# Two-layer transformer backbone: the first two token pairs of the second layer are normalised and transposed during the first layer's attention and parked in DRAM

## The chip, the cores and the metric

The kernel runs on one core of a Trainium2 chip. The metric is the device time of one execution in microseconds (us); of several executions the median is taken.

## The reference

The reference is a backbone of two layers over 256 context tokens and 1024 latent tokens, each 1024 wide. Layer 0 is a windowed attention, layer 1 a latent attention. Cut to what matters here, with layer 1's input normalisation in the first line of the loop:

```python
for i in range(DEPTH):                       # DEPTH = 2
    hx = rms_norm(x, norm_g[i]) * (1.0 + scale_x) + shift_x
    hc = rms_norm(ctx, norm_g[i]) * (1.0 + scale_c) + shift_c
    yx, yc = window_gqa(hx, hc, ...) if i == 0 else latent_attention(hx, hc, ...)
    x = x + gate_x * yx
    if i < DEPTH - 1:
        ctx = ctx + gate_c * yc
return rms_norm(x, final_g)
# latent_attention begins with
cq, ckv, kr, g = split(h @ w_in)             # for the latent and the context tokens
```

All arithmetic is in float32. Products on TensorE (PE) are made from operands split into a high and a low part: the helper mm3 (L124 to L128) issues three matmuls for one product, and the helper split (L119 to L122) makes the parts, a cast on ScalarE (ACT, L121) and a subtraction (L122) on VectorE (DVE) or GpSimd (POOL).

## The kernel before

The 1280 tokens are ten tiles of 128, called t0 to t9 here; t0 and t1 are the context, and two neighbouring tiles are a pair (p0 is t0 and t1, p4 is t8 and t9). Most of SBUF is two arenas, arena_f (plain numbers) and arena_r (split operands), in which every stage has fixed places, given in KB per partition. A ring is a list of such places that are taken in turn; whoever takes a place waits until its last user is done.

**Layer 0's attention** runs in 40 units, one for each tile and each of 4 head groups, in the tile order 2, 0, 3, 1, 4, 5, 6, 7, 8, 9. A unit's work is written out by hand: scores (PE, L586), masked and reduced on DVE (L597), exponentials on ACT (L600), transposes of the probabilities through the two PSUM banks 6 and 7 (PE, L617), a split of what was transposed (L121, L122), the product with V (PE, L627), and a normalisation of the unit's output (L637 to L654, fin and fin2, whose transposes are L646). Behind four units stands the output product of their tile, outproj: mm3 calls that are handed out piece by piece inside the next tile's units, then L674 and L675, and the finished tile goes to DRAM in x1_d (L676). The last tile's outproj has no unit left to hide in and runs after the last unit.

**Layer 1's beginning** (from the line fetch1(0, nc.vector) on) makes its inputs from x1_d. For a tile, norm_x loads it (L212), squares and sums it on ACT (L214), makes the reciprocal root in three small steps (L215 DVE, L216 POOL), and scales it (L217 DVE); turn_x transposes it in eight 128x128 blocks on PE (L224), four to a PSUM bank, and copies the two banks out on ACT (L225). For a pair, build_h applies the layer's scale and shift (L238 DVE, eight a pair), and splits it (L241 ACT, L243 DVE) into hT1, the operand of the products. Then kv_tile computes each tile's key/value latents, 24 matmuls over 288 columns, with a squared sum on ACT (L958), small steps (L959 DVE, L960 POOL), a scaling on DVE (L997), and, two tiles later, a transpose and a split of the result (L1010, L121, L122), and g_tile(6, p) a part of the gates, 48 matmuls over 256 columns.

The weights come through a staging ring of three places, stg: fetch1 loads a piece (L264), splits it (L121, L122), and only then may the place be loaded again. Block 0 (the kv weights, eight pieces of 144 KB) is split by ACT and DVE, blocks 6 and 1 (four pieces of 256 KB each, here W6 and W1) by ACT and POOL. All loads named here are issued by the SP queue, in its order: an issue that must wait for a place holds up those behind it.

The program text gives the order of effects; a scheduler puts the instructions of the five engines into queues of its own choosing, up to the second layer's attention, whose PE, ACT and DVE order is written by hand. In such a queue nothing overtakes.

Of the kernel before, what the change touches and what calls it, by code (L numbers as in the profile page):

```python
# [18 lines left out]
D = 1024  # L19
# [41 lines left out]
def kernel(ctx: ExitStack, tc: tile.TileContext, t, out, dbg=None):  # L61
# [14 lines left out]
    x1_d = dpool.tile([TOK, D], F32, name="x1_d")  # L76
    qn_d = dpool.tile([8, 128, 2, SEQ], F32, name="qn_d")
# [132 lines left out]
    def norm_x(src, xr, junk):  # L210
        x = xr.next()
        load(out=x, in_=src)  # L212
        st = sm_ring()
# [4 lines left out]
        return x  # L218

    def turn_x(x, xt, j):  # L220
        for q in range(2):
            ps = shp(pst(), 4, 128)
            for c in range(4):
                nc.tensor.transpose(ps[:, c, :], x[:, (4 * q + c) * 128 : (4 * q + c + 1) * 128], ident)  # L224
            nc.scalar.copy(xt[:, 4 * q : 4 * q + 4, j * 128 : j * 128 + 128], ps)  # L225

    def build_x(p, src, xr, xtr, junk):

        xt = shp(xtr.next(), 8, 256)
        for j in range(2):  # L230
            turn_x(norm_x(src(2 * p + j), xr, junk), xt, j)
        return xt

    def build_h(p, xt, hT, A, B, fast=False, ks=range(8)):

        w = 1 if p == 0 else 0
        for k in ks:
            nc.vector.tensor_scalar(xt[:, k, :], xt[:, k, :], A[:, k, w : w + 1], B[:, k, w : w + 1], ALU.mult, ALU.add)  # L238
            if k % 2:
                hi = hT[:, 0, k - 1 : k + 1, :]  # L240
                nc.scalar.copy(hi, xt[:, k - 1 : k + 1, :])  # L241
                eng = nc.vector if fast or k % 4 == 1 else nc.gpsimd
                eng.tensor_sub(hT[:, 1, k - 1 : k + 1, :], xt[:, k - 1 : k + 1, :], hi.bitcast(F32))  # L243
# [434 lines left out]
    units = [UnitA(ti, g) for ti in ORDER for g in range(4)]  # L678

# [193 lines left out]
    for ui, u in enumerate(units):  # L873
# [11 lines left out]
        for ci in range(u.m):  # L885
# [215 lines left out]
    for ti in range(NT):  # L1101
        n = ti + 3
        if 4 <= n < NT:
            if n % 2 == 0:
                xt = shp(xtr.next(), 8, 256)
# [16 lines left out]
    qst = Ring(F, [16, 20, 24, 37, 41, 45], 1024)  # L1122
# [553 lines left out]
```

## Time and profile before

| what | us |
|---|---|
| median of 3 executions (1597.37 to 1597.9) | 1597.49 |
| profiled execution, its own time | 1596.15 |
| its span, first to last instruction | 1594.4 |
| around the span | 1.75 |

PE is busy for 1555.2 us of the span (98%), DVE for 905.9, ACT for 777.0 and POOL for 742.1. The mean granted PE clock is 0.997 of full speed. Layer 0's attention lies at about 360 to 716 us, layer 1's beginning after it. In the rows of the timeline the first number is the start in us from the span's start, the second the time in us of the instructions that the row merges, and a bracket gives the idle time before it and what ended that. Matmuls overlap, so that the distance from row to row, not the time in a row, is what a matmul takes.

### The profile page before, as it was taken

To read this page: it belongs to the slowest core of one execution; us is meant where nothing else is said; L and a number is where in the kernel's file an instruction comes from. 1 tells how busy PE (TensorE), PEld (TensorE's weight loads), DVE (VectorE), ACT (ScalarE), POOL (GpSimd) and SP (SyncE) were. 2 spreads that over 40 slices of the span, in tenths; PEclk is the share of its full clock that TensorE was granted. 3 is DMA by queue.
4 is the path that set the end of the run, shared out by engine and by line. 5 is a ranking of instruction groups with operands and counts; after the bars stand their busy time and mean duration, and the time that the engine had idled before them with its cause. 6 is when DMAs were issued, how large, how long until landed. Compare 5 with 4: busy or idle time off the path is not lost.

```text
span 1594.4 us, 26916 instructions
## 1 busy us (share of the span) xinstructions
PE 1555.2 (98%) x9938; PEld 1222.6 (77%) x9938; DVE 905.9 (57%) x1629; ACT 777.0 (49%) x1478; POOL 742.1 (47%) x805
## 2 busy tenths in 40 slices
PE   7899999999999999998999999999999999999998
PEld 4787777887878888887998899766766766766687
DVE  3515551618777777768525302667677677667454
ACT  3522232348777777767523332455545555555322
POOL 1231112115664444454113350388688688689510
PEclk9999999999999999999999999999999999999999
DMA  7446776354333333327113753313232233244251
GB/s 253 166 138 196 233 210 190 97 153 120 109 110 94 97 93 94 93 79 244 35 34 106 262 184 94 103 30 101 69 96 80 76 88 96 67 130 118 67 167 66
DMA packets 147203, 192.82 MB, mean 121 GB/s; under 512 B 13936, under 2 KB 84080, under 8 KB 147072
## 3 DMA queue, kind: packets, MB, share of 16 engines
q1 hardware_dynamic: 145456, 188.94, 39.5%
q10 hardware_dynamic: 1616, 2.17, 0.5%
q8 instruction: 78, 1.28, 0.4%
q14 instruction: 53, 0.43, 0.1%
HBM read 144.90 MB, written 46.15 MB: 120 GB/s over the span
## 4 chain that ended last, share of the span: by engine, by line
PE 86%; issue 2%; DVE 2%; POOL 2%; ACT 2%; DMA 1%; SPq 0%; POOLq 0%; DVEq 0%; ACTq 0%
PE PB L126 15%; PE PB L127 14%; PE PB L128 14%; PE PB L1303 11%; PE PB L1325 8%; PE PB L586 5%; PE PB L627 4%; PE PB L1266 4%; PE PB L617 4%; PE PB L183 1%; PE PB L1274 1%; PE PB L1354 1%; PE PB L646 1%; ACT arena_r L121 1%; DVE arena_r L122 1%
## 5 line engine op out<-in xcount | busy, mean ns | idle before, releaser
L126 PE MATMUL PB<-arena_r 128*128 128x512 f32 (+3 forms) x1496 | 509.9, 342 | 4.9 <-POOL arena_r L653 2.0
L127 PE MATMUL PB<-arena_r 128*128 128x512 f32 (+3 forms) x1496 | 502.4, 336 | 4.2 <-DVE arena_r L390 2.1
L128 PE MATMUL PB<-arena_r 128*128 128x512 f32 (+3 forms) x1496 | 500.3, 335 | 0.3 <-DVE arena_r L122 0.3
L1317 POOL TENSOR_TENSOR arena_f<-arena_f 128x512 f32<-128x512 f32 x252 | 328.3, 1303 | 82.1 <-ACT arena_f L1309 65.3
L126 PEld LDWEIGHTS PB<-arena_r 128*128 128x128 f32 x1496 | 283.7, 190 | 52.7 <-issue 12.5
L127 PEld LDWEIGHTS PB<-arena_r 128*128 128x128 f32 x1496 | 284.5, 190 | 32.0 <-DVE arena_r L390 3.5
L128 PEld LDWEIGHTS PB<-arena_r 128*128 128x128 f32 x1496 | 284.5, 190 | 28.3 <-DVE arena_r L122 0.5
L122 POOL TENSOR_TENSOR arena_r<-arena_f,arena_r 128x512 fp32r<-128x512 f32 x88 | 115.2, 1325 | 299.7 <-ACT arena_r L121 255.5
L1309 ACT ACTIVATE arena_f<-PB 128x1024 f32<-128x1024 f32 x160 | 164.1, 1027 | 108.9 <-PE PB L1303 65.9
L1268 DVE TENSOR_REDUCE arena_f<-PB 128x1 f32<-128x1024 f32 x128 | 156.1, 1219 | 86.7 <-PE PB L1266 86.6
L1303 PE MATMUL PB<-arena_r 64*128 64x512 f32 (+1 forms) x1600 | 202.3, 392 | 0.3 <-ACT arena_f L1309 0.3
L1303 PEld LDWEIGHTS PB<-arena_r 64*128 64x128 f32 (+1 forms) x1600 | 146.1, 185 | 31.5 <-ACT arena_f L1309 1.8
L122 DVE TENSOR_TENSOR arena_r<-PB,arena_r 128x512 fp32r<-128x512 f32 (+1 forms) x186 | 124.2, 674 | 61.9 <-ACT arena_r L121 61.0
L1325 PE MATMUL PB<-arena_f 128*64 128x512 f32 x640 | 144.4, 597 | 0.0
L600 ACT ACTIVATE arena_f<-arena_f,small 128x640 f32<-128x640 f32 (+2 forms) x160 | 119.5, 747 | 35.4 <-DVE small L597 32.7
L597 DVE CUSTOM_DVE_ANT_0 arena_f<-PB,arena_f,small 128x640 f32<-128x640 f32 (+2 forms) x176 | 125.2, 722 | 20.1 <-PE PB L586 12.6
L121 ACT CAST arena_r<-PB 128x512 fp32r<-128x512 f32 (+1 forms) x186 | 105.3, 573 | 47.4 <-PE PB L617 45.2
L121 ACT CAST arena_r<-arena_f 128x512 fp32r<-128x512 f32 (+3 forms) x141 | 83.8, 603 | 86.7 <-PE PB L128 12.5
L627 PE MATMUL PB<-arena_r 128*128 128x512 f32 x336 | 115.8, 429 | 0.5 <-DVE arena_f L639 0.5
L586 PE MATMUL PB<-arena_r 128*128 128x256 f32 (+1 forms) x576 | 111.0, 308 | 1.6 <-DVE small L597 1.3
L1325 PEld LDWEIGHTS PB<-arena_f 128*64 128x64 f32 x640 | 43.1, 136 | 83.2 <-issue 79.9
L617 PE MATMUL PB<-ident,arena_f 128*128 128x128 f32 x672 | 104.2, 274 | 1.3 <-DVE arena_r L122 0.8
(177 smaller groups left out, 1842.9 us busy)
## 6 DMA issues: line engine op xcount, KB each, us to landing
arena_f<-ada_w SPq DMA_DIRECT2D x47, 512.0 KB, 5.4
arena_r<-q_d SPq DMA_DIRECT2D x80, 256.0 KB, 3.9
arena_r<-qn_d SPq DMA_DIRECT2D x64, 256.0 KB, 3.9
arena_r<-qr_d SPq DMA_DIRECT2D x192, 64.0 KB, 3.3
arena_f<-a_w_in SPq DMA_DIRECT2D x40, 256.0 KB, 3.6
arena_f<-x SPq DMA_DIRECT2D x16, 512.0 KB, 6.6
g_d<-arena_f SPq DMA_DIRECT2D x32, 256.0 KB, 2.1
q_d<-arena_f SPq DMA_DIRECT2D x64, 128.0 KB, 2.4
```

What stands on the lines that cost most here:

```text
L121: nc.scalar.copy(hi, src)
L122: (lo_eng or nc.vector).tensor_sub(lo, src, hi.bitcast(F32))
L126: nc.tensor.matmul(o, ah, bh, start=first, stop=False)
L127: nc.tensor.matmul(o, al, bh, start=False, stop=False)
L128: nc.tensor.matmul(o, ah, bl, start=False, stop=last)
L586: nc.tensor.matmul(S[:, at : at + n], qT[:, s, hq, :], kT[:, g, k : k + n], start=s == 0, stop=s == 1)
L617: nc.tensor.transpose(pt[:, h, :], self.Ps[h][:, ci * 128 : ci * 128 + 128], ident)
L627: nc.tensor.matmul(self.pv, V[:, self.chunks[ci], self.g, :], PT[:, s], start=ci == 0 and s == 0, stop=ci == self.m - 1 and s == 1,)
L1303: nc.tensor.matmul(S[:, t], k[r, c : c + 128], q[r], start=j == 0, stop=j == 4)
L1309: nc.scalar.activation(E, self.S, AF.Exp)
L1317: eng.tensor_add(self.acc, self.acc, E[:, t])
L1325: nc.tensor.matmul(self.pv[p : p + 64], Vq[:, cs[t], self.h % 4, :], E[:, t], start=i == 0, stop=i == 4)
```

## The change

The first two pairs (t0 to t3) no longer go through norm_x and turn_x in layer 1. A generator, pre_turns, does the same work during layer 0's attention, tile by tile, four steps a tile and one step after each of the units 20 to 35 (tiles t5 to t8 of the attention); the results go to DRAM (xT_d), and load_xt brings them back, pair 0 during unit 38, pair 1 at the beginning of layer 1. In between, several rings are moved: layer 0's gr, or1 and rtr, layer 1's stg (its third place from 49.5 to 34 KB), xr, junk and the ring xtr, which becomes two fixed pairs of places, xt_at. The same instructions as before stay for pairs 2, 3 and 4.

```diff
+    xT_d = dpool.tile([2, 128, 8, 256], F32, name="xT_d")
...
-    or1, rtr = (Ring(F, [o, o - 5], 256) for o in (43, 45))
+    or1, rtr = Ring(F, [43, 44], 256), Ring(F, [45, 41], 256)
-    gr = Ring(F, [2.5, 34, 46], 256)
+    gr = Ring(F, [34, 35, 46], 256)
...
+    xpre, tpre = f_at(48, 1024), [f_at(o, 4, 128) for o in (36, 38)]
+    def pre_turn(ti):
+        load(out=xpre, in_=x1_d[ti * 128 : ti * 128 + 128, :])
+        yield
+        st = sm(4)
+        nc.scalar.activation(f_at(36, 512).bitcast(BF16), xpre, AF.Square, accum_out=st[:, 0:1])
+        nc.gpsimd.tensor_scalar(st[:, 1:2], st[:, 0:1], 1.0 / D, EPS, ALU.mult, ALU.add)
+        nc.gpsimd.tensor_tensor(st[:, 2:3], st[:, 1:2], mhalf, ALU.pow)
+        yield
+        nc.vector.tensor_scalar_mul(xpre, xpre, st[:, 2:3])
+        yield
+        for q in range(2):
+            ps = shp(pst3(), 4, 128)
+            for c in range(4):
+                k = 4 * q + c
+                nc.tensor.transpose(ps[:, c, :], xpre[:, k * 128 : k * 128 + 128], ident)
+            nc.scalar.copy(tpre[q], ps)
+            ts = slice(ti % 2 * 128, ti % 2 * 128 + 128)
+            load(out=xT_d[ti // 2, :, 4 * q : 4 * q + 4, ts], in_=tpre[q])
+        yield
+    xt_at = [[f_at(o, 4, 256) for o in os] for os in ((48, 36), (14, 18))]
+    def load_xt(p):
+        for q in range(2):
+            load(out=xt_at[p][q], in_=xT_d[p, :, 4 * q : 4 * q + 4, :])
...
+        if 20 <= ui < 36:
+            next(pre)
+        if ui == 38:
+            load_xt(0)
...
-    junk = f_at(34.5, 512).bitcast(BF16)
-    stg = Ring(F, [30, 32.25, 49.5], 576)
-    xr = Ring(F, [22, 26, 45], 1024)
-    xtr = Ring(F, [14, 37], 2048)
+    junk = f_at(40, 512).bitcast(BF16)
+    stg = Ring(F, [30, 32, 34], 512)
+    xr = Ring(F, [22, 26, 42], 1024)
...
     fetch1(0, nc.vector)
-    xts = {0: build_x(0, src1, xr, xtr, junk)}
-    build_h(0, xts.pop(0), hT1[0], ada1.A, ada1.B, fast=True)
-    xts[1] = build_x(1, src1, xr, xtr, junk)
-    build_h(1, xts.pop(1), hT1[1], ada1.A, ada1.B, fast=True)
+    load_xt(1)
+    build_h(0, xt_at[0], hT1[0], ada1.A, ada1.B, fast=True)
+    build_h(1, xt_at[1], hT1[1], ada1.A, ada1.B, fast=True)
```

The scheduler lays the queues anew. In the changed kernel the helpers' lines are one further on (the cast of split is L122, its subtraction L123) and norm_x and turn_x stand at L213, L219 to L222 and L228, L229. Three places matter for what follows.

On ACT, behind the last unit, before the change: the casts of the kv weights (L121, 128x288) alternate with the squares (L214) and the copies of the transposed tiles (L225) of t0 to t3; the squares are those of t0, t1 and t2.

```order
L121 CAST arena_r<-arena_f 128x288 x3
L214 ACTIVATE arena_f<-arena_f 128x1024 x2
L121 CAST arena_r<-arena_f 128x288 x2
L225 COPY arena_f<-PB 128x4x128
L121 CAST arena_r<-arena_f 128x288
L225 COPY arena_f<-PB 128x4x128 x2
L214 ACTIVATE arena_f<-arena_f 128x1024
```

On ACT at the same place with the change: the first square (L219) is t4's, the second t5's, and between them stand the last kv weights, the copies of t4, the first two casts of W6 (L122, 128x512) and the squared sum of kv tile 0 (L993).

```order
L122 CAST arena_r<-arena_f 128x288 x2
L219 ACTIVATE arena_f,small<-arena_f 128x1024
L122 CAST arena_r<-arena_f 128x288 x5
L1006 DMA arena_f<-b_q_norm 128x512
L122 CAST arena_r<-arena_f 128x288
L229 COPY arena_f<-PB 128x4x128 x2
L1008 DMA arena_f<-b_kv_norm 128x256
L122 CAST arena_r<-arena_f 128x512 x2
L993 ACTIVATE arena_f,small<-PB 128x256
L219 ACTIVATE arena_f,small<-arena_f 128x1024
L122 CAST arena_r<-arena_f 128x512
```

So t0 to t3 are gone from ACT's queue there, t4 has moved to the front, and t5 stands behind two weight casts that wait for transfers.

On SP with the change, from the end of unit 38 on: the loads of the turned pair 1 (L708), then the tiles t4, t5 and t6 (L213) between the pieces of the kv weights (L263, 128x288), the store of t8 of layer 0 (L675), the reload of t9 for the last output product (L657) and the first two pieces of W6 (L263, 128x2x256).

```order
L708 DMA arena_f<-xT_d 128x1024 x2
L213 DMA arena_f<-x_d 128x1024
L263 DMA arena_f<-b_w_in 128x288 x2
L213 DMA arena_f<-x_d 128x1024
L675 DMA x_d<-arena_f 128x1024
L263 DMA arena_f<-b_w_in 128x288 x3
L657 DMA arena_f<-x 128x1024
L213 DMA arena_f<-x_d 128x1024
L263 DMA arena_f<-b_w_in 128x288 x3
L263 DMA arena_f<-b_w_in 128x2x256 x2
```

Before the change the tiles loaded in this stretch were t0 to t4, and one piece of the kv weights stood much farther ahead, in front of the store of an earlier tile; now all eight stand here.

On ACT in the attention, at unit 23 and alike at units 27, 31 and 35, the copies of a turned tile (L695) stand right behind the unit's own output copies (L636) and ahead of its exponentials (L599), of the next output copy (L647) and of the next cast of transposed probabilities (L122).

```order
L636 COPY arena_f<-PB 64x256 x2
L695 COPY arena_f<-PB 128x512 x2
L599 ACTIVATE arena_f,small<-arena_f,small 128x640
L647 COPY arena_f<-PB 128x256
L122 CAST arena_r<-PB 128x512
```

Before, the cast of transposed probabilities that now follows later stood in the place of L695.

More of the change, by code (lines that the diff above doesn't have):

```diff
@@ L224, in turn_x @@
                 nc.tensor.transpose(ps[:, c, :], x[:, (4 * q + c) * 128 : (4 * q + c + 1) * 128], ident)
[L225 to L232, printed above, removed]
+            nc.scalar.copy(xt[q][:, :, j * 128 : j * 128 + 128], ps)
     def build_h(p, xt, hT, A, B, fast=False, ks=range(8)):
@@ L1103 @@
         if 4 <= n < NT:
-            if n % 2 == 0:
-                xt = shp(xtr.next(), 8, 256)
+            xt = xt_at[n // 2 % 2]
             turn_x(nx, xt, n % 2)
```

18 lines of the change are left out of this document (13 added, 5 removed).

## The prediction

> **What bounds the kernel now.** I read the table of busy time first, for three stretches: the change's old place (716.3 to 764.4 us, from the last unit's end to the start of kv tile 4), its new place, and what comes next. Columns: stretch, its length, busy us of PE, PEld, DVE, ACT and POOL with counts, PE clock, DMA share, GB/s.
>
> ```profile
> 716.30:764.40 48.10, 40.34 (x262) 35.88 (x260) 40.63 (x92) 36.51 (x76) 20.78 (x24) 0.96 0.69 217
> 580.00:700.00 120.00, 119.59 (x723) 102.57 (x722) 91.44 (x187) 87.74 (x206) 60.62 (x105) 1.00 0.30 87
> 764.40:840.00 75.60, 75.60 (x621) 75.60 (x620) 28.17 (x81) 22.77 (x57) 10.10 (x20) 1.00 0.10 31
> ```
>
> PE bounds both neighbours: it idles 0.41 of 120 us in the attention and never from 764.4 to 840. Only the middle stretch has holes: 48.10 - 40.34 = 7.76 us, at a clock of 0.96. So a shift of kv tile 4's start goes through to the end. Then I read PE's timeline there.
>
> ```profile
> 722.02 1.09 PE L224 MATMUL PB<-ident,arena_f 128*128 128x128 f32 x8 [0.50 <-DVE small L215]
> 730.47 0.29 PE L126 MATMUL PB<-arena_r 128*128 128x288 f32 x1
> 734.66 1.06 PE L224 MATMUL PB<-ident,arena_f 128*128 128x128 f32 x8 [0.90 <-DVE arena_f L217]
> 744.60 0.40 PE L126 MATMUL PB<-arena_r 128*128 128x288 f32 x1 [1.12 <-ACT arena_r L241]
> 745.55 0.40 PE L127 MATMUL PB<-arena_r 128*128 128x288 f32 x1 [0.55 <-DVE arena_r L243]
> 748.52 1.09 PE L224 MATMUL PB<-ident,arena_f 128*128 128x128 f32 x8 [1.24 <-DVE small L959]
> 752.49 0.28 PE L126 MATMUL PB<-arena_r 128*128 128x256 f32 x1
> 754.63 0.28 PE L126 MATMUL PB<-arena_r 128*128 128x256 f32 x1
> 758.23 0.69 PE L1010 MATMUL PB<-ident,arena_f 128*128 128x128 f32 x2 [3.31 <-ACT arena_f L225]
> 758.57 0.56 PE L127 MATMUL PB<-arena_r 128*128 128x256 f32 x1
> 761.06 0.31 PE L126 MATMUL PB<-arena_r 128*128 128x256 f32 x1
> 764.46 0.38 PE L126 MATMUL PB<-arena_r 128*128 128x288 f32 x1
> ```
>
> The six waits make 7.62 us. The first three and the fourth (0.50, 0.90, 1.12, 0.55) wait for t0 to t3, which the change takes away: 3.07 us. The last two, 4.55 us, wait for t5 and for a PSUM bank that t6 holds; those tiles stay. After the 3.31 us wait 11 matmuls take 2.49 us (0.226 each) where 18 of the same shape took 2.14 just before (0.119): a slow stretch that costs about 1.2 us.
>
> The Trainium skill, "TensorE: Matmul & The Clock Gate", Part 1, says that about 3.4 us without work halve PE's clock and that about 3.4 us of work restore it. Here 3.31 us of waiting sufficed, and the slow stretch was nearer 2.5 us; by the rule each long wait would cost 1.7 us instead of the measured 1.2, and the sum below 0.5 more.
>
> **The change part by part.** Prices come from the chain of waits (first two rows: start, us) and from the groups of that stretch (busy us, then mean ns of one).
>
> ```profile
> 763.84 0.87 PE PB L224 x8
> 764.71 0.13 PE PB L126
> L214 ACT ACTIVATE arena_f<-arena_f 128x1024 bf16<-128x1024 f32 x9 | 9.5, 1059 | 0.7 <-DMA arena_f<-x_d 0.5
> L214 ACT ACTIVATION_READ_ACCUMULATOR arena_f<-arena_f 128x1 f32 x9 | 1.7, 189 | 0.0
> L225 ACT COPY arena_f<-PB 128x512 f32<-128x512 f32 x15 | 8.5, 582 | 2.4 <-PE PB L224 2.4
> L121 ACT CAST arena_r<-arena_f 128x512 fp32r<-128x512 f32 x8 | 4.8, 620 | 0.0
> L958 ACT ACTIVATE arena_f<-PB 128x256 bf16<-128x256 f32 x4 | 1.5, 385 | 0.1
> L217 DVE TENSOR_SCALAR arena_f<-arena_f,small 128x1024 f32<-128x1024 f32 x9 | 6.8, 753 | 4.4 <-POOL small L216 4.4
> L216 POOL TENSOR_TENSOR small<-small 128x1 f32<-128x1 f32 x9 | 5.5, 608 | 10.1 <-DVE small L215 9.2 <-DVE small L959 0.8
> L122 POOL TENSOR_TENSOR arena_r<-arena_f,arena_r 128x512 fp32r<-128x512 f32 x8 | 10.9, 1377 | 7.8 <-ACT arena_r L121 6.5 <-DMA arena_f<-b_q_norm 1.3
> ```
>
> *PE work, moved.* 4 tiles x 0.87 = 3.5 us leave the old place and go into the attention, where PE has 0.41 us free in 120: none fits. +3.5 us there.
>
> *Handling in the attention.* Each tile adds to ACT a square (1.06 + 0.19) and two copies (2 x 0.58), to DVE a scaling (0.75), to POOL a power (0.61) and a tiny scaling that the trace doesn't show, to SP a load and two stores (behind them wait the reload for outproj and the next g load; both are wanted a unit or more later). ACT and DVE are busy for 88 and 91 of 120 us there, so they have room, but the copies stand ahead of the cast of the next probabilities. Bounds: nothing, or all of ACT's and DVE's 3.16 us on PE's path. I take 0.3 a tile, near the lower end, since PE's whole idle time per unit there is 0.035 us: +1.2 us. Part of build_h also moves into the last two units' DVE and ACT queues; at nothing, since the row below shows a hole of 2.89 us on DVE there; without it, up to five L238 of 0.34 = 1.7 us.
>
> *The extra trip through DRAM.* The stores come long before the loads, and pair 0 is loaded in unit 38: hidden.
>
> *The old place, walked.* The walk leaves the attention's delay out and keeps the times of the trace above. The first two rows below are transfers (KB, median us from issue to landing), the rest timeline.
>
> ```profile
> arena_f<-x_d SPq DMA_DIRECT2D x8, 512.0 KB, 6.0
> arena_f<-b_w_in SPq DMA_DIRECT2D x11, 256.0 KB, 4.5
> 725.21 0.38 SPq L264 DMA_DIRECT2D arena_f<-b_w_in  x1
> 730.78 0.62 ACT L121 CAST arena_r<-arena_f 128x512 fp32r<-128x512 f32 x1
> 723.84 0.80 SPq L264 DMA_DIRECT2D arena_f<-b_w_in  x2
> 727.59 0.43 ACT L121 CAST arena_r<-arena_f 128x288 fp32r<-128x288 f32 x1 [0.20 <-DMA arena_f<-b_w_in]
> 709.45 0.69 DVE L122 TENSOR_TENSOR arena_r<-PB,arena_r 128x512 fp32r<-128x512 f32 x1 [2.89 <-ACT arena_r L121]
> 779.38 1.71 DVE L238 TENSOR_SCALAR arena_f<-arena_f,small 128x256 f32<-128x256 f32 x5 [4.37 <-ACT arena_f L225]
> 751.16 5.60 DVE L238 TENSOR_SCALAR arena_f<-arena_f,small 128x256 f32<-128x256 f32 x8
> 750.94 4.05 POOL L122 TENSOR_TENSOR arena_r<-arena_f,arena_r 128x512 fp32r<-128x512 f32 x3
> ```
>
> 1. kv tile 0 began at 730.47. Without the 16 transposes of t0 and t1 (1.7), the 0.50 wait and 0.5 for the gaps around those groups, too short for the table (about 0.16 a group, my choice), with t4's in front (0.9): 728.7. Its last weights come about when they did (staging as in the rows at 723.84 and 727.59): no wait. Tiles 0 and 1 and two matmuls more, 50 x 0.133: PE wants t5 at 735.3.
> 2. t5's square stands behind the casts of W6's first two pieces and tile 0's squared sum. The second piece can be loaded once the seventh kv piece is split, about 729.4 (cast near 728.4, as the row at 727.59 is the first of two, then two short DVE steps behind outproj's): + 4.5 = 733.9, cast 734.5, squared sum (0.39 + 0.19) 735.1, square (1.25) 736.4. POOL meanwhile subtracts W6's two pieces, to 736, then does tile 0's power; DVE's step for t5 stands behind tile 0's scaling: 737.5. Power (0.61), 0.1, scaling (0.75): transposes at 739.0. **A new wait of 3.7 us**, and a slow stretch, 1.2.
> 3. Transposes 0.9, 32 matmuls and a small transpose: 745.5, when t6's first half is ready too (its square waits for a cast of W1's first piece, in a place free at 736: + 4.5 + 0.6 + copy 0.6 + square 1.25 = 743, then DVE's L238 and power and scaling). No wait.
> 4. 16 kv and 7 gate matmuls and t6: about 749.5. t6's second half needs the bank that tile 0's result leaves; DVE leaves it behind tile 2's scaling, whose power POOL does behind W1's last piece (place free 742.7, + 4.5, cast 0.6, subtraction 1.4: 749.2), then about 1.9 of small steps: 751.1. A wait of 1.6.
> 5. 0.4 + 36 x 0.119 + 0.9: kv tile 4 at 756.7; with 0.8 for the gaps around five transpose groups, at 757.5.
>
> Gain: 764.46 - 757.5 = 7.0 us. Bounds: 764.46 - 750.5 = 14, if no wait is left (728.7 + 96 x 0.133 + 48 x 0.119 + 3.5); and 3.8, if each of the three transfers in a row (steps 2 and 4) takes 725.21 to 730.78, 5.6 us, thus 3 x 1.07 = 3.2 more.
>
> L238 takes 0.34 alone (five in 1.71) and 0.70 beside POOL's subtractions (eight in 5.60, POOL busy for 4.05). If W6's third subtraction meets t5's scaling, the wait grows by up to 1.38 us; it lies in the range.
>
> On this the Trainium skill, "SBUF — State Buffer", section "SBUF: two separate sides", has DVE and POOL share one port pair under an exclusive lock, the loser blocked for the whole instruction. The trace agrees in the main: full blocking would make those eight 4.05 + 8 x 0.34 = 6.8 us, 5.60 are measured. By the rule the sum would be 1.4 us worse.
>
> *Sum.* -7.0 + 3.5 + 1.2 = -2.3 us: the profiled execution's 1596.15 (span 1594.4) becomes 1593.9. It lies 1.3 below the median of 1597.49; for the median I say **1595.2 us**.
>
> **The rivals.** 0.2% is 3.2 us, about what a measurement of this kernel tells from no change: below 1594.3 is faster, above 1600.7 slower.
>
> *A, the forecast, 0.5*: the hole moves from t0 to t3 over to t5 and the weights; 1592.5 to 1598.
>
> *B, the holes go, 0.2.* If W6's pieces land early enough that t5's square is done before 733, the wait, its slow stretch and step 4's wait fall away: 764.46 - 751.5 = 13, less 4.7: 1589.2. For it: PE alone needs only that long, and t5's load is issued right behind the first two kv pieces and takes 6.0 us, so t5 lies ready long before. Against it: ACT's order with the casts in front.
>
> *C, the attention pays, 0.17.* The copies and the square hold up ACT's casts of probabilities, so that both PSUM banks of the transposes stay full and PE stands. At the full 3.16 us a tile: + 12.6 + 3.5 - 7.0 = +9.1: 1606.6. It decides slower from 1.7 us a tile on ((3.2 + 7.0 - 3.5) / 4). For it: ACT and DVE wait for each other there all the time. Against it: both are a quarter idle.
>
> *D, slow weights, 0.13.* Transfers at 5.6 us: gain 3.8 only, +0.9: 1598.4.
>
> That the change doesn't do what it says is ruled out by the order: the transposes do stand in units 23, 27, 31, 35.
>
> **How the numbers follow.** The likeliest is A. About 0.16 of A's 0.5 lies below 1594.3, with B 0.36 faster. C gives 0.17 slower, and a little of D: 0.18. The rest, 0.46, is the same. The range, 1589.5 to 1601, takes in A, D and about half of B and leaves out most of C and the other half of B, some 0.2.
>
> **What would show it.** On PE, transposes of t5 (L228) with a wait of 3 to 5 us before them, released by a small DVE or POOL step, at the end of the table's middle stretch; before kv tile 0 no wait. From the last unit to kv tile 4, 41 us instead of 48. From 580 to the last unit's end, 4.7 us more. I am wrong in step 2 if PE runs through kv tiles 0 to 3, and in the attention's price if the 16 units grow by less than 3 or more than 7 us.

## The result, and the profile after

| kernel | executions | median us | ratio to the kernel before, 95% interval |
|---|---|---|---|
| before | 6 | 1597.70 (1596.71 to 1599.46) | |
| changed | 6 | 1612.76 (1607.08 to 1614.58) | 1.0086 [1.0067, 1.0104] |

The change makes the kernel 0.9% slower, where 1595.2 was forecast in a range up to 1601.0. The profiled execution was the fastest of the six (1607.08, span 1605.3), so the spans differ by 10.9 us and the medians by 15. The executions' granted PE clock goes with their time: 0.995 in the two fastest, 0.991 to 0.993 in the other four.

I cut both profiles at the same three events: the closing transposes (L645, before the change L646) of unit 19 and of unit 39, and the last transposes of t9 in layer 1 (L228, L224). Ahead of the first cut the two traces agree (525.55 and 525.63 us), behind the last they take 816.3 and 816.4 us. All of the difference lies in between. First the kernel before, by busy time per stretch: the attention's last 20 units by tiles, then the old place. Columns as in the prediction: stretch, length, busy us of PE, PEld, DVE, ACT and POOL with counts, PE clock, DMA share, GB/s.

```profile
525.63:565.93 40.30, 40.23 (x240) 34.61 (x241) 30.96 (x63) 29.52 (x69) 19.90 (x34) 1.00 0.32 92
565.93:606.23 40.30, 40.24 (x240) 34.65 (x241) 30.97 (x63) 29.45 (x69) 19.91 (x34) 1.00 0.33 92
...
686.07:716.14 30.07, 29.72 (x173) 24.92 (x174) 20.28 (x44) 19.83 (x49) 16.87 (x29) 1.00 0.21 68
716.14:778.01 61.87, 54.11 (x371) 49.65 (x370) 49.16 (x118) 43.31 (x91) 23.16 (x29) 0.97 0.56 176
```

The same stretches of the changed kernel:

```profile
525.55:566.55 41.00, 40.37 (x240) 34.65 (x241) 31.52 (x64) 30.66 (x72) 20.71 (x36) 1.00 0.33 95
566.55:611.17 44.62, 41.77 (x250) 35.25 (x250) 31.53 (x64) 31.33 (x73) 20.69 (x36) 1.00 0.35 107
...
698.65:730.94 32.29, 31.08 (x183) 25.97 (x182) 28.78 (x63) 24.62 (x58) 17.92 (x29) 1.00 0.48 152
730.94:788.99 58.05, 51.08 (x340) 48.07 (x339) 37.39 (x91) 30.36 (x67) 20.51 (x25) 0.94 0.47 149
```

The old place became 3.8 us shorter (61.87 to 58.05). The attention became 14.9 us longer (190.51 to 205.39). In the second row PE is busy 1.5 us more than before and idle 2.85 us instead of 0.06. These are PE's long waits in the changed kernel's timeline, first in the attention, then in the old place:

```profile
580.19 0.85 PE L585 MATMUL PB<-arena_r 128*128 128x256 f32 x4 [2.78 <-DVE small L596]
624.55 0.85 PE L585 MATMUL PB<-arena_r 128*128 128x256 f32 x4 [2.55 <-DVE small L596]
668.39 0.85 PE L585 MATMUL PB<-arena_r 128*128 128x256 f32 x4 [2.01 <-DVE small L596]
...
745.04 0.40 PE L127 MATMUL PB<-arena_r 128*128 128x288 f32 x1 [1.12 <-DVE arena_f L673]
753.60 1.94 PE L228 MATMUL PB<-ident,arena_f 128*128 128x128 f32 x8 [2.32 <-DVE arena_f L222]
763.56 1.02 PE L228 MATMUL PB<-ident,arena_f 128*128 128x128 f32 x4 [3.19 <-ACT arena_r L122]
769.84 0.66 PE L228 MATMUL PB<-ident,arena_f 128*128 128x128 f32 x4 [0.34 <-DVE small L220]
```

The three waits in the attention have one form: scores (L585) wait for the mask step on DVE (L596). What holds DVE shows when the queues are read back from there. The same timeline, SP first, then ACT, POOL and DVE:

```profile
566.34 1.03 SPq L697 DMA_DIRECT2D xT_d<-arena_f  x2
568.04 1.71 SPq L657 DMA_DIRECT2D arena_f<-x  x1
569.84 0.39 SPq L569 DMA_DIRECT2D arena_f<-g_d  x1
570.33 0.41 SPq L681 DMA_DIRECT2D arena_f<-x_d  x1
...
575.87 1.06 ACT L684 ACTIVATE arena_f<-arena_f 128x1024 bf16<-128x1024 f32 x1 [2.21 <-DMA arena_f<-x_d]
577.11 0.19 POOL L685 TENSOR_SCALAR small<-small 128x1 f32<-128x1 f32 x1 [3.89 <-ACT arena_f L684]
577.38 0.56 POOL L686 TENSOR_TENSOR small<-small 128x1 f32<-128x1 f32 x1
577.98 0.75 DVE L688 TENSOR_SCALAR arena_f<-arena_f,small 128x1024 f32<-128x1024 f32 x1 [3.60 <-POOL small L686]
...
579.25 0.88 DVE L596 CUSTOM_DVE_ANT_0 arena_f<-PB,arena_f,small 128x640 f32<-128x640 f32 x1
```

The load of the next tile (L681) has one place, so it must wait for the last tile's transposes; in SP's queue it then stands behind two stores, the reload for outproj and a g load. Issued at 570.33, it is waited for until 575.87, 5.5 us later. Its square stands at the head of ACT's queue 2.21 us before that. DVE comes to the scaling (L688) early too and stands 3.60 us for it, with the mask step for PE's scores (L596) behind it. So a late transfer goes through three in-order queues to PE.

### The profile page after: what moved, and what is told of

Read it like the earlier page. It is cut to its first block, busy times and chain, and to the rows that moved or that the text cites. A ratio compares the mean times of both kernels' runs of the same rounds, so it can differ in the third digit from the quotient of the medians.

```text
span 1605.3 us, 26934 instructions
## 1 busy us (share of the span) xinstructions
PE 1559.7 (97%) x9938; PEld 1226.3 (76%) x9938; DVE 892.5 (56%) x1625; ACT 776.1 (48%) x1478; POOL 746.9 (47%) x809
## 3 DMA queue, kind: packets, MB, share of 16 engines
q10 hardware_dynamic: 1616, 2.17, 0.5%
## 4 chain that ended last, share of the span: by engine, by line
PE 84%; DMA 4%; DVE 3%; issue 3%; POOL 3%; ACT 2%; SPq 0%; POOLq 0%; ACTq 0%; DVEq 0%
PE PB L127 15%; PE PB L128 14%; PE PB L129 14%; PE PB L1336 11%; PE PB L1358 8%; PE PB L1299 4%; PE PB L585 4%; PE PB L626 3%; PE PB L616 3%; PE PB L184 2%; DMA arena_f<-x_d 1%; PE PB L1307 1%; DMA arena_f<-b_w_in 1%; DVE arena_r L123 1%; PE PB L1387 1%
## 5 line engine op out<-in xcount | busy, mean ns | idle before, releaser
L123 POOL TENSOR_TENSOR arena_r<-arena_f,arena_r 128x512 fp32r<-128x512 f32 x88 | 115.5, 1327 | 305.1 <-ACT arena_r L122 264.8
L123 DVE TENSOR_TENSOR arena_r<-PB,arena_r 128x512 fp32r<-128x512 f32 (+1 forms) x186 | 123.6, 673 | 53.7 <-ACT arena_r L122 52.8
L599 ACT ACTIVATE arena_f<-arena_f,small 128x640 f32<-128x640 f32 (+2 forms) x160 | 119.6, 748 | 39.0 <-DVE small L596 37.3
L596 DVE CUSTOM_DVE_ANT_0 arena_f<-PB,arena_f,small 128x640 f32<-128x640 f32 (+2 forms) x176 | 125.2, 722 | 22.8 <-PE PB L585 16.2
L122 ACT CAST arena_r<-arena_f 128x512 fp32r<-128x512 f32 (+3 forms) x141 | 83.9, 603 | 99.0 <-DMA arena_f<-b_w_in 21.5
L122 ACT CAST arena_r<-PB 128x512 fp32r<-128x512 f32 (+1 forms) x186 | 105.3, 573 | 40.7 <-PE PB L616 37.1
L585 PE MATMUL PB<-arena_r 128*128 128x256 f32 (+1 forms) x576 | 113.2, 310 | 8.9 <-DVE small L596 8.7
```

Source lines behind the costliest of these rows:

```text
L122: nc.scalar.copy(hi, src)
L123: (lo_eng or nc.vector).tensor_sub(lo, src, hi.bitcast(F32))
L585: nc.tensor.matmul(S[:, at : at + n], qT[:, s, hq, :], kT[:, g, k : k + n], start=s == 0, stop=s == 1)
```

## The experiments

Each ratio is to executions of the kernel before on the same chip, whose medians lie between 1597.28 and 1598.26 us, so that ratios compare better than medians. The two lengths come from the profiles, cut as above.

| label | median us | ratio, 95% interval | attention us | old place us |
|---|---|---|---|---|
| before | 1597.7 | | 190.51 | 61.87 |
| changed | 1612.76 | 1.0086 [1.0067, 1.0104] | 205.39 | 58.05 |
| e1_square_kept | 1599.72 | 1.0016 [1.0007, 1.0025] | 198.05 | 58.20 |
| e2_rings_only | 1596.15 | 1.0001 [0.9992, 1.0010] | 190.59 | 61.97 |
| e3_turn_twice | 1612.47 | 1.0097 [1.0083, 1.0110] | 204.19 | 63.43 |
| e4_kv_staging | 1607.97 | 1.0067 [1.0053, 1.0081] | 209.72 | 56.96 |
| e5_changed_again | 1611.89 | 1.0086 [1.0064, 1.0108] | 207.28 | 58.82 |
| e6_kvn_early | 1599.18 | 1.0003 [0.9994, 1.0011] | 197.64 | 56.93 |
| e7_square_t5_first | 1598.92 | 1.0012 [1.0002, 1.0022] | 198.25 | 56.89 |
| e8_h0_shared | 1600.71 | 1.0015 [1.0006, 1.0024] | 198.18 | 58.38 |
| e9_squares_t5_t6 | 1599.34 | 1.0013 [1.0004, 1.0022] | 197.92 | 58.12 |
| e10_order_alone | 1598.09 | 0.9996 [0.9987, 1.0005] | 190.62 | 64.50 |
| e11_w1_late | 1599.27 | 1.0005 [0.9996, 1.0014] | 197.74 | 55.72 |
| e12_w1_late_no_turn | 1598.08 | 0.9999 [0.9990, 1.0008] | 190.47 | 62.59 |
| e13_w1_late_t5_first | 1599.63 | 1.0010 [1.0002, 1.0019] | 197.70 | 57.47 |
| e14_scaling_late | 1596.25 | 0.9991 [0.9982, 1.0001] | 195.55 | 55.77 |
| e15_pair0_late | 1599.24 | 1.0007 [0.9998, 1.0015] | 197.02 | 57.92 |
| e16_both_late | 1596.96 | 0.9997 [0.9987, 1.0006] | 195.19 | 56.62 |
| e17_best | 1595.95 | 0.9988 [0.9979, 0.9997] | 195.66 | 55.04 |
| e18_best_staging | 1593.14 | 0.9973 [0.9963, 0.9983] | 195.79 | 53.27 |

### The attention: the wait, the work or the rings

**e1_square_kept.** keep_in_program_order leaves an instruction in its engine's queue where the program text has it; below this is called pinned. issue_after, used further on, puts instructions behind another one in their engine's queue.

```diff
-        nc.scalar.activation(f_at(36, 512).bitcast(BF16), xpre, AF.Square, accum_out=st[:, 0:1])
+        tc.keep_in_program_order(nc.scalar.activation(f_at(36, 512).bitcast(BF16), xpre, AF.Square, accum_out=st[:, 0:1]))
```

> One line differs from the changed kernel: the square of the early-turned tiles (L684) is pinned in ACT's queue behind what the program text puts before it, about 13 us later than where the scheduler put it; the same instructions are done. Theory W (the wait): the attention pays because the square stands in ACT's queue sooner behind the load of its tile than that load takes, so ACT, then DVE, then PE stand. Then PE's waits of 2.78, 2.55 and 2.01 us in the attention go, the last unit's end (730.94) comes at 722 to 725, and the time falls from 1612.8 by 6 to 10 us, to about 1604, still above the 1597.7 of the kernel before. Theory C (the work: squares, copies and scalings hold up ACT and DVE, wherever they stand): the last unit's end stays within 2 us of 730.9 and the time within 3 us of 1612.8.

Measured: 1599.72, 13 us below the changed kernel by the medians, 11 by the ratios, where 6 to 10 were expected. In its timeline the load is followed by the square 18.7 us later, with no wait on ACT; DVE's wait for the scaling is 1.01 us instead of 3.60:

```profile
572.38 0.41 SPq L681 DMA_DIRECT2D arena_f<-x_d  x1
...
591.10 1.05 ACT L684 ACTIVATE arena_f<-arena_f 128x1024 bf16<-128x1024 f32 x1
593.20 0.75 DVE L688 TENSOR_SCALAR arena_f<-arena_f,small 128x1024 f32<-128x1024 f32 x1 [1.01 <-POOL small L686]
...
750.34 1.93 PE L228 MATMUL PB<-ident,arena_f 128*128 128x128 f32 x8 [3.68 <-DVE arena_f L222]
759.09 0.63 PE L228 MATMUL PB<-ident,arena_f 128*128 128x128 f32 x4 [1.90 <-DVE arena_f L222]
```

The stretch that took 44.62 us now takes 41.75, of which PE is idle for 0.18:

```profile
568.97:610.72 41.75, 41.57 (x249) 35.18 (x249) 31.74 (x64) 31.40 (x73) 21.09 (x36) 1.00 0.39 114
```

The same instructions are done and the three waits are gone, so theory C falls and W holds. The attention's loss goes from 14.9 to 7.5 us. The old place is as long as in the changed kernel; its waits for t5 and t6 stay (last two rows of the timeline).

**e2_rings_only and e3_turn_twice** undo one half each.

```diff
# e2: nothing turned in the attention
-        if 20 <= ui < 36:
-            next(pre)
-        if ui == 38:
-            load_xt(0)
...
-    load_xt(1)
+    for j in range(2):
+        turn_x(norm_x(src1(j), xr, junk), xt_at[0], j)
...
# e3: e2, and the early turning runs unused
+        if 20 <= ui < 36:
+            next(pre)
```

> Nothing is turned in the attention and nothing goes through the extra DRAM tile: t0 to t3 are normalised and turned in layer 1 as before, but all rings stand where the change puts them (staging 30, 32, 34; the moved gr, or1, rtr, xr, junk and the two fixed places for the turned pairs). Theory W and C: the attention ends at 716 as before (within 0.5 us), and the time is 1597.7 within 3 us. Theory R (the moved places cost): 3 us or more above 1597.7, either inside the attention (gr, or1, rtr) or behind it, where the third staging place, 49.5 before, is now free only when the attention ends.

> The early turning runs in the attention as in the changed kernel, and its result is not used: layer 1 turns t0 to t3 at the old place as before, on the changed rings. It prices the attention alone. If the attention's loss of 14.8 us and the old place's gain of 3.6 us, as the two profiles have them, are both right and independent: the attention ends near 731 and the time is 1612.8 + 3.6 = about 1616, 14 to 20 us above the kernel before. If part of the 14.8 us came from the old place's work drawn into the attention (loads of the turned pair, its scaling and shifts), the attention ends earlier, at 724 to 728.

Measured: e2 is the kernel before in both lengths (190.59, 61.97) and in time, so the moved rings cost nothing and theory R falls. e3 loses 13.7 us in the attention and 1.6 behind it: nearly all of the attention's loss belongs to the early turning. Its last four units take 31.03 us, in the changed kernel 32.29, before 30.07: some 1.3 us of the changed kernel's loss come with layer 1's work drawn into those units. All sixteen scalings of pairs 0 and 1 (L236) stand there in the changed kernel, from 707.8 to 728.3 us; in e3 and before they come behind the last unit. e3's time misses the 1616 expected: by the ratios it is 1.8 us above the changed kernel, not 3.6.

**e5_changed_again** is the changed kernel once more.

> The changed kernel once more, for its spread: its six executions reached from 1607.1 to 1614.6 and the profile was taken in the fastest of them, so that the 10.9 us between the two spans explain 11 of the 15 us between the medians. Theory W, as the first experiment left it (waits of 2 to 3 us for the load, and slow matmuls behind some of them): a profile of an execution near 1612.8 shows the same three waits in the attention, longer or with a slower clock behind them, and the rest of the kernel as long as before. If the missing 4 us lie behind 780 us, they have another cause.

Measured: 1611.89. Its profiled execution took 1611.49. Against the first profile the part ahead of the early turning is 1.8 us longer, the attention 1.9, the old place 0.8, the rest as long. The waits are not what differs: the three in the attention are shorter here (1.76, 2.46 and 1.60 us). The PE clock differs. It is 0.50 in this trace for 3.41 us from 401.35, ahead of the early turning, and again from 582.26 and 626.63, behind two of the waits; in the first profile it is 1.00 in the attention and around 401. Half the clock for 3.41 us costs up to 1.7. So, by this trace, the difference between the first profile and the median is a matter of the clock. Two profiles of one kernel differ by 0.8 us in the old place and 1.9 in the attention, so that a smaller difference between two runs' lengths shows little.

### The old place: why 3.8 us and not 7.0

**e4_kv_staging.**

```diff
-    fetch1(0, nc.vector)
+    fetch1(0, nc.vector, Ring(F, [2.5, 30, 32, 34], 288))
```

> The changed kernel, with four staging places for the kv weights alone (a place at 2.5 KB that is free all through the attention, and 30, 32, 34), so that one piece is loaded long ahead and one more place turns over. If the old place gave 3.6 us instead of 7 because the weights come late there, the stretch from the last unit's end to kv tile 4 falls from 44.7 us to 41 to 43 and the time by 2 to 4 us; if it is the order of the queues (squares behind casts), it stays within 1 us. The attention should stay at 730.9.

Measured: the old place falls by 1.1 us (58.05 to 56.96), less than the 2 to 4 us expected; the ratio falls from 1.0086 to 1.0067 (3 us, with overlapping intervals), though the profiled attention was 4.3 us longer. Its three waits (3.10, 1.88 and 2.62 us) sum to 0.3 us more than the changed kernel's, but behind the first and the last the PE clock is 0.50 for 3.41 and 6.83 us. The weights' arrival is at most a share of the old place's waits: 1.1 us is little more than the 0.8 by which two profiles of the changed kernel differ.

**e6_kvn_early and e7_square_t5_first** (both on e1).

```diff
# e6
-    kvn = f_at(10, 256)
+    kvn = f_at(46, 256)
...
+    load2(out=kvn, in_=t["b_kv_norm"].partition_broadcast(128))
     load2(out=cosb, ...
# e7: e6, and
-    fetch1(6)
+    nxs = [norm_x(src1(n), xr, junk) for n in (4, 5)]
+    with tc.issue_after(norm_x.sq.ins):
+        fetch1(6)
```

> The first experiment's kernel (square pinned), with the norm weights of the key/value latents (kvn) loaded to a place that is free before the last output product ends, so that kv tile 0's scaling (L1031, 2.48 us behind that load in the first experiment's profile) no longer holds up DVE's queue, in which t5's small step stands behind it. If that load is what makes PE wait for t5 there (3.68 us), the wait falls to about 1.7 and the time by 2 to 3 us, to 1597; if it is t5's square behind W6's casts, as the prediction had it, the wait stays within 0.7 us of 3.7 and the time within 1 us of 1599.7.

> As the one before, and t5's square pinned ahead of W6's casts in ACT's queue (the square of t5 then stands right behind that of t4). The prediction's step 2 says that t5 waits because its square stands behind the casts of W6's first two pieces and tile 0's squared sum: then with this the wait before t5's transposes goes altogether (below 0.3 us), the next late thing is t6 (its halves waited 1.90 and 1.91 us), and the time falls by 2 to 4 us against the kernel with the early kvn, to 1593 to 1596, below the kernel before (1597.3). If t6 takes all of it back, it stays within 1 us.

Measured, e6's timeline of PE, then e7's:

```profile
745.46 1.06 PE L228 MATMUL PB<-ident,arena_f 128*128 128x128 f32 x8 [1.96 <-DVE arena_f L222]
754.58 1.09 PE L228 MATMUL PB<-ident,arena_f 128*128 128x128 f32 x4 [3.85 <-DVE arena_f L222]
```

```profile
755.51 1.09 PE L228 MATMUL PB<-ident,arena_f 128*128 128x128 f32 x4 [4.97 <-DVE arena_f L222]
```

With the early norm weights t5's wait falls from 3.68 to 1.96 us, so that in e1 1.7 us of it came from that load, and t6's grows to 3.85. With t5's square ahead of W6's casts t5 has no wait left, which shows that place in the queue to be what step 2 of the prediction took it for: the casts come 16.5 us behind the last unit, in e6 16.4, while t5's square, and with it its scaling, has moved ahead of them. t6 takes the gain back. The old place is 56.9 us in both; e7's time is 0.3 us below e6's by the medians and 1.4 above it by the ratios.

**e8_h0_shared**, on e7: `fast=True` is left out for pair 0 in build_h.

> As the one before, with one in two of pair 0's subtractions (L242) moved from DVE to POOL, which is idle from 729 to 743 us. The prediction put the part of build_h that moves into the last two units at nothing; the last four units are 2.2 us longer in the changed kernel and 2.7 in the first experiment than before. If DVE's load there is the cause, those units come down by about 1 us and the time too; if not (PE's own work of t3 and the copies), it stays within 0.7 us of the kernel one step before.

Measured: the last four units stay (32.93 us for 32.97), the time is 1600.71, 1.8 us above e7 by the medians and 0.5 by the ratios. The half of pair 0's subtractions that the edit gives to POOL is not what lengthens those units. The old place is 1.5 us longer.

**e9_squares_t5_t6**, on e7.

```diff
-    load2(out=qn, in_=t["b_q_norm"].partition_broadcast(128))
+    ld = load2(out=qn, in_=t["b_q_norm"].partition_broadcast(128))
...
+    with tc.issue_after(ld.ins):
+        nxs.append(norm_x(src1(6), xr, junk))
```

> As the kernel with t5's square first, and the load, square and scaling of t6 (then t7 in turn) put one tile earlier in the text, t6's square pinned behind the kv weights and ahead of W6's casts: t6's scaling (L222) then stands in DVE's queue ahead of pair 2's eight L236, which in the experiment before it stand between t5's transposes and t6's, beside POOL's subtractions. If this order is what keeps the old place's gain at 3.4 to 3.6 us instead of the predicted 7.0, the wait of 4.97 us before t6's first half falls below 1 us, the stretch from the last unit's end to kv tile 4 falls from about 45 us to about 41, and the time from 1599 to about 1595. If the weights or the copies' bank hold PE there, another wait of 3 us or more takes its place and the time stays within 1 us of 1599.

Measured: 1599.34, the second case. t6's first half waits 0.57 us, and two new waits stand behind it:

```profile
756.56 0.33 PE L1048 MATMUL PB<-ident,arena_f 128*128 128x128 f32 x1 [3.21 <-ACT arena_f L229]
759.86 1.12 PE L228 MATMUL PB<-ident,arena_f 128*128 128x128 f32 x4 [2.97 <-DVE arena_r L123]
```

With each order the wait turns up in another place.

**e10_order_alone**: e7's last two edits on e2, no early turning.

> No early turning: the kernel with the rings moved alone, with the norm weights of the key/value latents loaded early and W6's casts pinned behind t5's square. There the wait before t5's transposes is 3.12 us, behind POOL's subtractions of W6 and W1 and kv tile 0's small steps; with W6 later POOL is free for them. If the order of these queues is worth something by itself, the wait goes and the time falls from 1596.2 to 1592 to 1594; if the wait only moves to W6's gate products or to t6, it stays within 1.5 us of 1596.2. Either way it says what the early turning must beat.

Measured: 1598.09, the old place 64.50 us, 2.5 longer than in e2. With t0 to t3 still there, t5's load comes too late for its square to go first; ACT stands for it, as it did in the attention:

```profile
740.31 1.06 ACT L219 ACTIVATE arena_f<-arena_f 128x1024 bf16<-128x1024 f32 x1 [2.25 <-DMA arena_f<-x_d]
```

**e11_w1_late (on e1), e12_w1_late_no_turn (on e2) and e13_w1_late_t5_first (on e7).**

```diff
     fetch1(6)
-    fetch1(1)
...
+        if ti == 4:
+            with tc.issue_after(norm_x.sq.ins):
+                fetch1(1)
         kv_tile(ti)
```

> The first experiment's kernel (square pinned, 1599.7) with one more edit: W1, the weights of block 1, which no product needs before the latent queries, is fetched in the text at kv tile 4, and its casts are pinned behind t8's square, so that ACT's four casts and POOL's four subtractions of W1 (1.3 us each, beside which DVE's instructions take twice as long) leave the stretch between the last unit and kv tile 4. In every kernel so far PE's waits there add up to 6.5 to 8.6 us, whoever releases them. If W1's handling feeds them (theory H: DVE, slowed by POOL, sets the pace there), the sum of the waits falls to 3 to 5 us and the time by 2 to 4 us, to about 1596. If it is the order of ACT's queue alone or the arrival of W6, the sum stays above 6 and the time within 1 us of 1599.7.

> The same late W1 in the kernel with the rings moved alone (no early turning, 1596.2). Theory H: the 3.12 us wait before t5, behind kv tile 0's power step that POOL does behind the weights' subtractions, falls below 1 us and the time by 2 to 4 us, to about 1593; what the early turning then adds is the difference to the kernel before this one. Otherwise within 1 us of 1596.2.

> Late W1, early norm weights and t5's square first, with the early turning and the pinned square: all that has been tried for the old place in one kernel. Theory H: t5 without a wait (as with its square first), and t6's first half, which waited 4.97 us behind DVE's eight L236 beside POOL, below 2.5 us; time 1594 to 1596, below the kernel before (1597 to 1598). If the waits again move on to the next tile, the sum in the stretch stays above 6 us and the time near 1599.

Measured: with the early turning the old place falls from 58.20 to 55.72 us (e13, 57.47, does worse than e7's 56.89). e11's remaining waits:

```profile
745.92 1.06 PE L228 MATMUL PB<-ident,arena_f 128*128 128x128 f32 x8 [2.05 <-DVE arena_f L222]
753.34 0.63 PE L228 MATMUL PB<-ident,arena_f 128*128 128x128 f32 x4 [2.80 <-ACT arena_r L122]
```

The old place now gives 6.2 us, near the 7.0 forecast. But the sum of its waits falls from 8.56 to 7.15 us only, where theory H had 3 to 5, and the time stays within 1 us by the medians: by the signs named ahead, H does not hold. Of the 2.5 us 1.4 are less waiting; besides, the PE clock is 1.00 throughout e11's old place and 0.97 in e1's. Without the early turning the same edit gives nothing (62.59). The medians of e11 and e1 differ by 0.5 us, the ratios by 0.0011, with overlapping intervals.

### What a tile costs in the attention

**e14_scaling_late and e15_pair0_late (both on e11), e16_both_late.**

```diff
# e14
-        nc.vector.tensor_scalar_mul(xpre, xpre, st[:, 2:3])
+        tc.keep_in_program_order(nc.vector.tensor_scalar_mul(xpre, xpre, st[:, 2:3]))
# e15
-    units[-1].fin2(fast=True)
+    lf = units[-1].fin2(fast=True)
...
+    with tc.issue_after(lf.ins):
+        build_h(0, xt_at[0], hT1[0], ada1.A, ada1.B, fast=True)
```

> The kernel with the pinned square and the late W1, and one more pin: the scaling of the early tiles (L688) stands in DVE's queue where the text has it, about a unit after the power step, instead of right behind the square, where DVE stood 1.01 us for POOL's result. In that kernel a tile turned in the attention costs 1.46 us (41.76 us for four units instead of 40.30), of which PE's own transposes are 0.87. If DVE's standing is the handling's price, a tile falls to 0.9 to 1.1, the attention's loss from about 7.1 to 5 to 6 us, and the time by 1 to 2 us against 1599.3; if the copies and ACT's order are, it stays within 0.15 us a tile.

> The kernel with the pinned square and the late W1, with DVE's scalings and subtractions of pair 0 (L236, L242 of build_h) pinned behind the last unit's closing steps, so that they no longer stand in the last two units. The prediction put that share at nothing, 1.7 us at most. If it costs, the last four units fall from 32.4 to 31.4 us or less (30.07 in the kernel before; t3's own transposes take 0.87); DVE then has more to do ahead of kv tile 0, and if that delays it, the stretch up to t9's transposes grows by as much. Time within 1.5 us of 1599.3 either way.

> Both of these pins in one kernel, as the version with everything that helped. If each gives its share: attention's loss 4 to 5 us, old place's gain 5 to 6, time 1596 to 1598, level with the kernel before (1597 to 1598) or just below; if the shares do not add up, 1598 to 1600.

Measured: the groups of the attention (busy us, mean ns, then idle time ahead and its releaser), first e1, whose queues are e11's there, then e14, and e14's stretch:

```profile
L688 DVE TENSOR_SCALAR arena_f<-arena_f,small 128x1024 f32<-128x1024 f32 x4 | 3.0, 753 | 4.1 <-POOL small L686 4.1
```

```profile
L688 DVE TENSOR_SCALAR arena_f<-arena_f,small 128x1024 f32<-128x1024 f32 x4 | 3.0, 752 | 0.0
```

```profile
570.73:611.94 41.21, 41.15 (x249) 35.48 (x248) 31.64 (x63) 31.64 (x73) 20.61 (x36) 1.00 0.41 116
```

DVE's 4.1 us of standing are gone, and a tile costs 41.21 - 40.30 = 0.91 us, which is PE's transposes (0.87) and nothing else. e14's time is 1596.25, 2.2 us below e11 by the ratios, with overlapping intervals. Pinning pair 0 (e15) takes 0.7 us off the last four units (32.53 to 31.84; the kernels that use the early turning without this pin take 32.2 to 33.0) and puts 2.2 on the old place. Pair 1's scalings, which it does not pin, still begin ahead of the last unit's end (715.1 of 723.7 us). In e16 the attention's loss is 4.7 us, the sum that the prediction had for it, by luck: 0.9 of the 1.2 us beside the transposes lie in the last four units, which the prediction had at nothing.

### A version that beats both

**e17_best** joins e14 with e6's early norm weights, **e18_best_staging** adds e4's staging.

> The edits that helped, in one kernel: square and scaling of the early tiles pinned, W1 late, the norm weights of the key/value latents early. Alone, the early norm weights shortened the stretch from the last unit to t9's transposes from 58.2 to 56.9 us, and the late W1 to 55.7. If the two add, the stretch is 54.5 us, the attention's loss 5 us as in the kernel with the pinned scaling, and the time about 1595, 2 to 3 us (0.15 to 0.2%) below the kernel before. If they hit the same wait, 1596 to 1597.

> The same with four staging places for the kv weights, which alone took 1.1 us off that stretch (56.96 for 58.05). If the weights' arrival is still among the waits, 1 us below the kernel beside it; if not, the same.

Measured: e17 0.9988, e18 0.9973 [0.9963, 0.9983]. e18's old place and the waits left in it:

```profile
722.83:776.10 53.27, 48.35 (x340) 44.98 (x339) 35.36 (x91) 30.48 (x67) 20.24 (x25) 1.00 0.51 161
```

```profile
744.39 1.06 PE L228 MATMUL PB<-ident,arena_f 128*128 128x128 f32 x8 [1.66 <-DVE arena_f L222]
750.05 0.63 PE L228 MATMUL PB<-ident,arena_f 128*128 128x128 f32 x4 [1.17 <-DVE arena_f L222]
```

The old place is 8.6 us shorter than before, the attention 5.3 longer: -3.3 us in the profiles, -4.3 by the ratio. Together the three edits to the old place take 4.9 us off e1's (58.20 to 53.27), as much as their lengths alone add up to (1.3, 2.5 and 1.1), while in the times of e6 and e11 little of it could be told from the noise.

## Why the prediction was wrong

**The step that failed** is "Handling in the attention", where I took 0.3 us a tile, +1.2 in all, from bounds of "nothing, or all of ACT's and DVE's 3.16 us on PE's path". In the profiled execution the loss beside PE's moved 3.5 us was 14.9 - 3.5 = 11.4 us, and in the second tile's stretch 44.62 - 40.30 - 0.87 = 3.45 us, above my upper bound. The bound counted the new instructions' busy time. It left out what they wait for: an instruction at the head of a queue costs its wait, not its length. By the runs the 11.4 us are: 7.3 for the load (e1), 2.2 for the scaling behind the power step (e14), and of the remaining 1.9, build_h's work in the last units is 0.7 (e15) to 1.3 (e3). The work itself costs 0.04 us a tile once nothing waits (e14). The 4 us by which the medians differ beyond the profiles went with the PE clock (e5), which the prediction had at 1.00 in the attention.

**"The extra trip through DRAM ... hidden"** held for the stores and for load_xt, for which only DVE waits, once, 0.6 us. For the load that starts a tile I asked who waits behind it on SP, and not what it waits behind nor who needs it how soon. The profile before had its time (6.0 us for a load from x_d), and the queues' new order its neighbours.

**PE work, moved, 3.5 us**: right (0.91 a tile in e14).

**Part of build_h in the last two units, at nothing, up to 1.7**: 0.7 to 1.3 us, inside the bound, where I took its lower end. The bound counted five scalings; sixteen stand in the last three units.

**The old place, gain 7.0 (bounds 3.8 to 14)**: 3.8 by the profile. Step 1 held: kv tile 0 began 12.1 us behind the last unit (12.6 in the walk). A wait of 1.12 inside it, behind outproj's DVE step, was missed. Step 2 held in kind: t5 waited 2.32 us (3.7 forecast), behind W6's casts, POOL's subtractions of them, and tile 0's power and scaling (first two rows below); e7, where t5's square goes first, takes the wait away. Step 3, "No wait" for t6, failed: 3.19 us. Two things end it 0.13 us apart (last two rows): t6's scaling on DVE, behind pair 2's steps and slowed beside POOL's subtractions, and a cast on ACT (L122) that frees a PSUM bank. In e7 the scaling ends t6's wait; with it moved (e9), a copy on ACT and a bank that a split (L123) leaves late take its part. Step 4's wait was 0.34 instead of 1.6.

```profile
748.30 2.55 POOL L123 TENSOR_TENSOR arena_r<-arena_f,arena_r 128x512 fp32r<-128x512 f32 x2 [9.40 <-ACT arena_r L122]
751.40 0.48 DVE L1031 SCALAR_TENSOR_TENSOR arena_f<-PB,small,arena_f 128x256 f32<-128x256 f32 x1 [1.87 <-POOL small L995]
...
761.66 1.75 DVE L222 TENSOR_SCALAR arena_f<-arena_f,small 128x1024 f32<-128x1024 f32 x1 [0.44 <-POOL small L221]
763.18 0.36 ACT L122 CAST arena_r<-PB 128x256 fp32r<-128x256 f32 x1
```

The sum of the waits hardly changed, 7.62 us before and 6.97 after. The change took away the work of t0 to t3 and not the waits, which are a chain through ACT, DVE and POOL that weights and norm loads feed (e6, e11, e17, e18). Rival B's 13 us were out of reach for one edit; e18 got 8.6 with three edits there.

**Rival C (0.17)** had the right sign, and its decisive point (1.7 us a tile beside the transposes) was passed: the second tile's 3.45 is twice that. Its mechanism was not the one: squares and copies hold nothing up when their input is there (e1). What came is a rival that I did not write: a transfer that is late for an early place in a queue.

## What to carry to other kernels

When work is moved into a stage that has no slack, compare for each moved instruction that reads a transfer the distance in its engine's queue from the transfer's earliest issue with the transfer's measured time; bound its cost by the wait, not by its busy time. A scheduler's place for it is a guess on transfer times: pin it later, and pin what stands behind its result too. Where a stretch has several waits on coupled queues, one edit moves the wait on, so that its price is not the wait it removes: read it from the length of the whole stretch, and take the waits away together before judging the change. Where executions differ in clock, look at the clock before a wait is blamed.

## What the runs showed of the hardware

A wait of 2.32 us was enough for a slow stretch. Behind it, in the changed kernel, eight transposes take 1.94 us (1.04 behind no wait), and the kv matmuls start 0.24 us apart, where they started 0.13 apart at 743:

```profile
743.36 0.29 PE L129 MATMUL PB<-arena_r 128*128 128x288 f32 x1
743.49 0.29 PE L127 MATMUL PB<-arena_r 128*128 128x288 f32 x1
...
755.58 0.44 PE L127 MATMUL PB<-arena_r 128*128 128x288 f32 x1
755.82 0.44 PE L128 MATMUL PB<-arena_r 128*128 128x288 f32 x1
```

The granted clock is 0.50 from 753.41 us on for 3.41 us and again from 763.65 for as long, behind the 3.19 us wait; that makes 0.94 for the old place. It is 1.00 in e18's, whose longest wait is 1.66 us. The Trainium skill, "TensorE: Matmul & The Clock Gate", Part 1, puts the halving at about 3.4 us without work; here less sufficed.

The length of a wait alone does not decide it: 2.78 us in the changed kernel's attention and 2.80 us in e11 left the clock at 1.00. The two slow stretches start 10.24 us apart, three times their length. Counted back in steps of 3.41 us from them, PE stands for 2.13 and 3.19 us in the step ahead of each, while the step's edge at 579.33 splits the wait of 2.78 us into 1.93 and 0.85. Over all the traces, from 60 us on, a step with 2.05 us or more of standing was followed by half the clock, one with 1.6 to 2.0 sometimes. This is read from the traces; no run tests it.

In e1, DVE's scaling of t6 took 1.75 us beside POOL's subtractions, 0.75 alone:

```profile
757.20 1.75 DVE L222 TENSOR_SCALAR arena_f<-arena_f,small 128x1024 f32<-128x1024 f32 x1 [0.45 <-POOL small L221]
...
757.13 1.26 POOL L123 TENSOR_TENSOR arena_r<-arena_f,arena_r 128x512 fp32r<-128x512 f32 x1
758.55 1.53 POOL L123 TENSOR_TENSOR arena_r<-arena_f,arena_r 128x512 fp32r<-128x512 f32 x1 [0.15 <-DMA arena_f<-b_w_in]
```

POOL's first row ends at 758.39, 0.56 us before DVE's, so that of DVE's 0.75 us at most 0.19 were done beside it: nearly full blocking. The last 0.40 us ran beside POOL's next row, which took 1.53 us. This is closer to the rule of "SBUF — State Buffer", section "SBUF: two separate sides", in the Trainium skill than the eight scalings in the prediction were.
